# Gate and up projections of the experts taken by pairs of units, weights side by side

## The chip, the cores and the metric

The kernel runs on one core of one Trainium2 chip. The metric is the device time of one execution in microseconds (us); the median of several runs counts. Engines are named as in the profile: PE is the matrix engine TensorE (PEld its weight loads), DVE is VectorE, ACT is ScalarE, POOL is GpSimd, SP is SyncE, which issues the DMAs here.

## The reference

Two layers of a decoder trunk over 16 + 256 tokens of width 1024. The change touches only the last sub-layer, a top-2-of-8 expert SwiGLU:

```python
def swiglu(h, w_gate, w_up, w_down):
    return (jax.nn.silu(h @ w_gate) * (h @ w_up)) @ w_down

def moe_swiglu(h, router_w, w_gate, w_up, w_down):
    ...
    for e in range(N_EXPERTS):
        out = out + gates[..., e:e + 1].astype(h.dtype) * swiglu(h, w_gate[e], w_up[e], w_down[e])
    return out
```

There are 8 experts, each with gate and up matrices of 1024 x 3584 and a down matrix of 3584 x 1024, all float32. The weights, read once, are most of the kernel's traffic.

## The kernel before

The expert stage is a loop over 56 steps `s` (8 experts `e`, 7 slices `f` of 512 hidden columns). Each expert works on up to 128 gathered tokens. The tokens are the stationary operand of every product (`XG[e]`, tile `xq`) and the weights are the moving one, 512 columns at a time. To come near float32 accuracy from products in the faster type fp32r, each operand is split in a high and a low part, and three products are summed: high x high, high x low, low x high.

The weights come through `Stream`. A DMA brings a `raw` tile of 128 x 2048 (1 MB) from `wm`, in the order in which the host laid them out. A **unit** is half of such a tile, 128 x 1024, that is two chunks `k` of 512 columns. For each unit ACT makes the high part `whi` (`high`, L141) and DVE the low part `wlo` (`split`, L153: raw minus high). The pool `hl` holds four buffers of each kind (`HLB = 4`), so the high part of unit n+4 is written where that of unit n stood and waits for PE's last product that reads it. `unit(u)` sees to it that u and the three units behind it are split, and returns u's two parts. It is called where PE's products are written; the calls set the order in which casts and subtractions stand among the other work of ACT and DVE. In this stage the order of each engine's instructions is that of the program text (`manual_schedule`).

One step before the change, for s > 0:

- `gate_up(s, 0)`: gate, four units, six products for each (two chunks, each L1495, L1496, L1497), into one PSUM tile `gu`.
- ACT: Silu of that tile into `sg` (L1601).
- `transp(hcur)`: four transposes of the step before (L1505), ACT copies them to `hh` (L1508, high part), DVE makes `hlw` (L1509, low part).
- `gate_up(s, 1)`: up, four units, into a second `gu`; DVE multiplies `sg` by it (L1606).
- `down(s - 1, ...)` twice: four units, L1524 to L1526, into the tiles `yp0` and `yp1`, which live for the seven steps of an expert.

At an expert's end `unload` copies `yp0` and `yp1` out (L1536 on ACT, L1537 on DVE), and `combine` adds them to the tokens in the next step. `bg` takes up such pieces of background work between products. In the last step of all, `st.depth` falls from 4 to 3, and ACT loads a table for the final root (`tabs`, L1609).

Of the kernel before, what the change touches and what calls it, by code (L numbers as in the profile page):

```python
# [8 lines left out]
F32 = mybir.dt.float32  # L9
# [3 lines left out]
AF = mybir.ActivationFunctionType  # L13
ALU = mybir.AluOpType
PSUM = bass.MemoryType.PSUM

P = 128
D = 1024
ND = 8
# [17 lines left out]
TW = 2048  # L37
UW = 1024
# [42 lines left out]
class Stream:  # L81
# [71 lines left out]
        nc.vector.tensor_tensor(lo, w, hi.bitcast(F32), op=ALU.subtract)  # L153
        self.units[u] = (hi, lo)

    def unit(self, u, last=None):
        v, n = u, 0
        while n < self.depth and v * UW < self.n * TW:
            if not self.is_raw(v):
                if self.lim < self.n and v // self.per >= NWF and v // self.per not in self.raw:  # L160
                    break
                self.split(v)
                n += 1
            v += 1
        for k in [k for k in self.units if k < u]:
            del self.units[k]
        for k in [k for k in self.raw if k < u // self.per - R1 - R2]:
            del self.raw[k]
        return self.units[u]
# [6 lines left out]
def trunk(ctx: ExitStack, tc: tile.TileContext, xt, pv, pw, cst, gfin, wf, wm, out, dbg=None):  # L176
    nc = tc.nc
    pe, act, dve, pool = nc.tensor, nc.scalar, nc.vector, nc.gpsimd
# [3 lines left out]
    ring1 = ctx.enter_context(tc.tile_pool(name="ring1", bufs=R1))  # L182
# [9 lines left out]
    def psum(tag, name):  # L192
        t = ps.tile([P, 512], F32, name=name, tag=tag)
        return t

    st = Stream(nc, ring1, hl, wf, wm)
# [115 lines left out]
    def bg(n):  # L312
        for _ in range(min(n, len(fill))):
            fill.pop(0)()
# [10 lines left out]
    with ExitStack() as mx:  # L325
# [52 lines left out]
        us = [fraw(B_S5, 8, raw_x(xf), NT)]  # L378
# [511 lines left out]
        for b in range(2):  # L890
            sg = slot(f"sg{b}")
# [31 lines left out]
    with ExitStack() as fx:  # L923
# [24 lines left out]
        for k0, k1 in ((0, 6), (6, 8)):  # L948
            for w in range(2):
                (hi, lo), o = first[w]  # L950
                for k in range(k0, k1):
                    c = k * P
# [54 lines left out]
    with ExitStack() as gx:  # L1007
# [329 lines left out]
        for m in range(8):  # L1337
            if m < 4:
                o = accs[m]
# [145 lines left out]
    def unit_base(s):  # L1485

        return 8 * s + 4 * max(0, s - 1)

    def gate_up(s, w):
        e = s // NF  # L1490
        o = psum("mm", "gu")
        for k in range(ND):
            hi, lo = st.unit(UM + unit_base(s) + 4 * w + k // 2)
            c = slice((k % 2) * 512, (k % 2) * 512 + 512)
            pe.matmul(o, XG[e][:, 0, k], hi[:, c], start=(k == 0), stop=False)  # L1495
            pe.matmul(o, XG[e][:, 0, k], lo[:, c], start=False, stop=False)  # L1496
            pe.matmul(o, XG[e][:, 1, k], hi[:, c], start=False, stop=(k == ND - 1))  # L1497
            if k % 2:
                bg(1)
        return o  # L1500

    def transp(h):
        tp = psum("x", "etp")
# [77 lines left out]
    for s in range(E * NF + 1):  # L1581
        last = s == E * NF
        e, f = divmod(s, NF)
        if s == 1:
            weigh()
        if s == 2 * NF:
            gft = const.tile([P, D], F32, name="gft", tag="gft")
            nc.sync.dma_start(gft, gfin[0:1].to_broadcast([P, D]))
        if s == E * NF - 1:
            st.depth = 3  # L1590
        if f == 1 and e:
            fill += [lambda d=d, i=i: combine(e - 1, d, i) for d in range(2) for i in range(2)]
        if e % 2 and e + 1 < E and f == 3:
            choose(e + 1)
            gather(e + 1)
        if f == 2 and not last:
            turn_choice(e)
        if not last:
            og = gate_up(s, 0)
            sg = ew.tile([P, 512], F32, name="sg")  # L1600
            act.activation(sg, og, AF.Silu)  # L1601
        if s and not last:
            ht = transp(hcur)
        if not last:
            ou = gate_up(s, 1)
            dve.tensor_tensor(sg, sg, ou, op=ALU.mult)  # L1606
            hcur = sg
        if s == E * NF - 1:
            act.activation(tabs, epst, AF.Sqrt)  # L1609
            down(s - 1, *ht, 0)  # L1610
            hn = transp(hcur)
            down(s - 1, *ht, 1)
            ht = hn
        elif last:
            down(s - 1, *ht, 0)
            unload(E - 1, 0)
            fill.append(lambda: [combine(E - 1, 0, i) for i in range(2)])
            down(s - 1, *ht, 1)
            gains(0)
            Ys[E - 1, 1] = [ew.tile([P, 512], F32, name="Yf", tag="xq2", bufs=1)]  # L1620
            act.activation(Ys[E - 1, 1][0], yps[E - 1, 1], AF.Copy)
        elif s:
            for d in range(2):
                down(s - 1, *ht, d)
                if s % NF == 0:
                    unload(e - 1, d)
# [10 lines left out]
    with tc.If(cnt > CAP):  # L1637
        pos2 = ep.tile([P, 2, 8], F32, name="pos2")
        dve.tensor_scalar(pos2, pos, -float(CAP), None, op0=ALU.add)
        for e in range(E):  # L1640
            ohs = ep.tile([P, 2, CAP], F32R, name="ohs2", tag="ohs", bufs=1)
            for i in range(2):
                dve.tensor_scalar(ohs[:, i], css("iota"), pos2[:, i, e:e + 1], None, op0=ALU.is_equal)
            tp = psum("x", "ohtp")
            for i in range(2):
                pe.transpose(tp[:, i * P:(i + 1) * P], ohs[:, i].bitcast(F32), ident)
            oht = ew.tile([P, 2, P], F32, name="oht2", tag="oht", bufs=1)
            act.activation(oht.rearrange("p i t -> p (i t)"), tp[:, :2 * P], AF.Copy)
            xe = ew.tile([P, 2, ND, CAP], F32, name="xe2", tag=f"xq{e % 2}", bufs=1)[:, 0]
            for k in range(ND):  # L1650
                gp_ = psum("x", "gp_")
                o = gp_[:, :CAP]
                for j in range(4):
                    w = (XL if j > 1 else XH)[:, j % 2, k * P:(k + 1) * P]
                    pe.matmul(o, w, ohs[:, j % 2], start=(j == 0), stop=(j == 3))
                act.activation(xe[:, k], o, AF.Copy)
            yp2 = [psum("mm", f"yp{d}") for d in range(2)]
            for f in range(NF):
                s = e * NF + f
                tg = unit_base(s) // 2  # L1660
                pair = []
                for w in range(2):
                    o = psum("mm", "gu")
                    for k in range(ND):
                        if k % 4 == 0:
                            rw = ring1.tile([P, TW], F32, name="raw2", tag="raw")
                            nc.sync.dma_start(rw, wm[tg + 2 * w + k // 4])
                        pe.matmul(o, xe[:, k], rw[:, (k % 4) * 512:(k % 4) * 512 + 512], start=(k == 0), stop=(k == 7))
                    pair.append(o)
                sg = ew.tile([P, 512], F32, name="sg")  # L1670
                act.activation(sg, pair[0], AF.Silu)
                dve.tensor_tensor(sg, sg, pair[1], op=ALU.mult)
                tp = psum("x", "etp")
                for j in range(4):
                    pe.transpose(tp[:, j * P:(j + 1) * P], sg[:, j * P:(j + 1) * P], ident)
                hh = ew.tile([P, 4, P], F32, name="hh2", tag="hh")
                act.activation(hh.rearrange("p j c -> p (j c)"), tp, AF.Copy)
                td = (unit_base(s + 1) + 8 if s + 1 < E * NF else unit_base(s + 1)) // 2
                for d in range(2):
                    rw = ring1.tile([P, TW], F32, name="raw3", tag="raw")  # L1680
                    nc.sync.dma_start(rw, wm[td + d])
                    for j in range(4):
                        pe.matmul(yp2[d], hh[:, j], rw[:, 512 * j:512 * j + 512], start=(f == 0 and j == 0),
                                  stop=(f == NF - 1 and j == 3))
            Y = ew.tile([P, 4, 512], F32, name="Y2", tag="Y", bufs=1)[:, :2]
            for d in range(2):
                act.activation(Y[:, d], yp2[d], AF.Copy)
            for i in range(2):
                for d in range(2):
                    o = psum("x", "cmb")  # L1690
                    pe.matmul(o, oht[:, i], Y[:, d], start=True, stop=True)
                    a = X[:, i, 512 * d:512 * d + 512]
                    dve.scalar_tensor_tensor(a, o, gat[:, i, e:e + 1], a, op0=ALU.mult, op1=ALU.add)

        sqs = ew.tile([P, 4, 512], F32, name="sqs", tag="xq0", bufs=1)
        gains(0)
        for d in range(2):
            squares(d)
        finish()


def _layout(inp):
# [85 lines left out]
    i = 0  # L1788
    for s in range(n + 1):
        if s < n:  # L1790
            wm[i:i + 2] = g[s]
            wm[i + 2:i + 4] = u[s]
            i += 4
        if s > 0:
            wm[i:i + 2] = d[s - 1]
            i += 2
# [40 lines left out]
```

## Time and profile before

| | |
|---|---|
| median of 3 runs | 1548.89 us (1548.7 to 1555.63) |
| the profiled execution's own time | 1549.66 us |
| span of its profile, first to last instruction | 1547.9 us |
| PE / PEld / DVE / ACT busy share of the span | 99% / 85% / 83% / 68% |
| DMA, mean over the span | 280 GB/s |
| first and last product of the expert stage begin at | 557.5 us and 1534.3 us |

The busy shares are averages over stages with different limits. The expert stage takes the last 64% of the span; it is the only one that the change touches, so it is read by itself below. A matmul's duration in the profile contains its drain, which lies under the next one: a row of 0.39 us does not mean that the next product starts 0.39 us later.

### The profile page before, as it was taken

The page shows a single profiled execution, that of the slowest core. Times are in us where ns is not written, and L with a number is a line of the kernel's source. Part 1 is how long each engine was busy: PE and PEld are TensorE (multiplying, and loading weights), DVE is VectorE, ACT ScalarE, POOL GpSimd, SP SyncE. Part 2 cuts the span into 40 slices and gives each one's busy share as a digit, 9 for nine tenths or more (in the row PEclk, how much of TensorE's full clock was granted, in tenths as well). Part 3 has the DMA queues.
Part 4 walks back from the last instruction along what each step waited for, and adds up shares of the span by engine and source line. Part 5 has one row for each costly group of instructions (what it writes and reads, how often), then busy time and mean ns, then how long its engine had stood idle before and what let it go on. Part 6 is the DMA issues. An engine that isn't in the chain of part 4 may idle for free.

```text
span 1547.9 us, 21948 instructions
## 1 busy us (share of the span) xinstructions
PE 1525.1 (99%) x8346; PEld 1321.7 (85%) x8346; DVE 1287.5 (83%) x1445; ACT 1048.5 (68%) x1265; POOL 134.9 (9%) x248
## 2 busy tenths in 40 slices
PE   9998999999999999999999999999999999999997
PEld 7888999999899988888888888888888888888885
DVE  6677676655595689999999999999999999999996
ACT  3345654444552587878787887777887787787875
POOL 8870100001200200000000000000000000000000
PEclk9999999999999999999999999999999999999998
DMA  7433555455336768999899999999999999999960
GB/s 249 140 100 113 170 188 185 166 176 179 109 137 238 279 250 322 372 364 355 337 382 347 375 372 353 342 377 355 364 363 368 347 352 354 376 375 361 356 240 29
DMA packets 69041, 434.09 MB, mean 280 GB/s; under 512 B 14400, under 2 KB 14784, under 8 KB 17216
## 3 DMA queue, kind: packets, MB, share of 16 engines
q1 hardware_dynamic: 68784, 432.35, 74.9%
q8 instruction: 67, 1.10, 0.3%
q14 instruction: 46, 0.38, 0.1%
q10 hardware_dynamic: 144, 0.26, 0.0%
HBM read 430.32 MB, written 1.05 MB: 279 GB/s over the span
## 4 chain that ended last, share of the span: by engine, by line
PE 86%; DVE 1%; issue 1%; ACT 1%; POOL 0%; DVEq 0%; ACTq 0%; POOLq 0%
PE gu L1495 13%; PE gu L1497 13%; PE gu L1496 13%; PE yp L1524 7%; PE yp L1526 7%; PE yp L1525 7%; PE acc L231 6%; PE acc L232 6%; PE acc L233 6%; PE etp L1505 2%; PE sc L1106 1%; PE acc L252 1%; PE wo L231 1%; PE wo L233 1%; PE wo L232 1%
## 5 line engine op out<-in xcount | busy, mean ns | idle before, releaser
L153 DVE TENSOR_TENSOR wlo<-raw,whi 128x1024 fp32r<-128x1024 f32 x788 | 948.9, 1223 | 124.0 <-ACT whi L141 86.6
L141 ACT ACTIVATE whi<-raw 128x1024 fp32r<-128x1024 f32 x788 | 825.7, 1060 | 277.3 <-PE gu L1497 100.6
L1495 PE MATMUL gu<-whi,xq 128*128 128x512 f32 x896 | 357.6, 399 | 0.6 <-ACT xq L1427 0.6
L1497 PE MATMUL gu<-whi,xq 128*128 128x512 f32 x896 | 351.4, 392 | 0.0
L1496 PE MATMUL gu<-wlo,xq 128*128 128x512 f32 x896 | 349.8, 390 | 0.0
L1497 PEld LDWEIGHTS gu<-whi,xq 128*128 128x128 f32 x896 | 168.2, 188 | 38.4 <-DVE xq L1428 0.2
L1496 PEld LDWEIGHTS gu<-wlo,xq 128*128 128x128 f32 x896 | 168.5, 188 | 34.7 <-DVE wlo L153 0.4
L1495 PEld LDWEIGHTS gu<-whi,xq 128*128 128x128 f32 x896 | 168.5, 188 | 33.9 <-ACT xq L1427 0.8
L1524 PE MATMUL yp<-whi,hh 128*128 128x512 f32 x448 | 176.0, 393 | 0.0
L1526 PE MATMUL yp<-whi,hlw 128*128 128x512 f32 x448 | 175.3, 391 | 0.0
L1525 PE MATMUL yp<-wlo,hh 128*128 128x512 f32 x448 | 174.8, 390 | 0.0
L231 PE MATMUL acc<-xg,whi 128*128 128x272 f32 (+1 forms) x576 | 167.9, 292 | 0.0
L233 PE MATMUL acc<-xg,wlo 128*128 128x272 f32 (+1 forms) x576 | 166.0, 288 | 0.4 <-DVE wlo L153 0.4
L232 PE MATMUL acc<-xg,whi 128*128 128x272 f32 (+1 forms) x576 | 165.3, 287 | 0.5 <-DVE xg L266 0.5
L231 PEld LDWEIGHTS acc<-xg,whi 128*128 128x128 f32 x576 | 108.5, 188 | 1.1 <-issue 0.6
L232 PEld LDWEIGHTS acc<-xg,whi 128*128 128x128 f32 x576 | 108.5, 188 | 0.9 <-DVE xg L266 0.7
L233 PEld LDWEIGHTS acc<-xg,wlo 128*128 128x128 f32 x576 | 108.4, 188 | 0.7 <-DVE wlo L153 0.6
L1526 PEld LDWEIGHTS yp<-whi,hlw 128*128 128x128 f32 x448 | 84.1, 188 | 19.0
L1525 PEld LDWEIGHTS yp<-wlo,hh 128*128 128x128 f32 x448 | 84.1, 188 | 18.5 <-DVE wlo L153 0.3
L1524 PEld LDWEIGHTS yp<-whi,hh 128*128 128x128 f32 x448 | 84.2, 188 | 17.4
L1566 POOL TENSOR_TENSOR ys<-X,gft 128x512 f32<-128x512 f32 x1 | 1.6, 1594 | 988.1 <-DVE X L1547 988.1
L252 PE MATMUL acc<-xfn,raw 128*128 128x272 f32 x320 | 78.2, 401 | 1.4 <-DMA raw<-in_wf_dram 0.7
(528 smaller groups left out, 1725.4 us busy)
## 6 DMA issues: line engine op xcount, KB each, us to landing
raw<-in_wm_dram SPq DMA_DIRECT2D x334, 1024.0 KB, 6.0
raw<-in_wf_dram SPq DMA_DIRECT2D x70, 1024.0 KB, 4.9
raw<-in_wm_dram SPq DMA_DIRECT2D x4, 512.0 KB, 6.4
hT<-in_xt_dram SPq DMA_DIRECT2D x4, 272.0 KB, 4.9
raw<-in_wf_dram SPq DMA_DIRECT2D x2, 512.0 KB, 5.3
out_dram<-ys SPq DMA_DIRECT2D x3, 256.0 KB, 4.1
KT<-k SPq DMA_DIRECT2D x10, 64.0 KB, 2.2
U<-uA SPq DMA_DIRECT2D x16, 34.0 KB, 2.1
```

The costliest lines, as they stand in the source:

```text
L141: self.nc.scalar.activation(hi, self.tile(i)[:, j * UW:(j + 1) * UW], AF.Copy)
L153: nc.vector.tensor_tensor(lo, w, hi.bitcast(F32), op=ALU.subtract)
L231: pe.matmul(o, wh, xh, start=start, stop=False)
L232: pe.matmul(o, wh, xl, start=False, stop=False)
L233: pe.matmul(o, wl, xh, start=False, stop=stop)
L252: pe.matmul(o, w[:, c:c + P], xs(k), start=(k == 0), stop=(k == nblk_k - 1))
L1495: pe.matmul(o, XG[e][:, 0, k], hi[:, c], start=(k == 0), stop=False)
L1496: pe.matmul(o, XG[e][:, 0, k], lo[:, c], start=False, stop=False)
L1497: pe.matmul(o, XG[e][:, 1, k], hi[:, c], start=False, stop=(k == ND - 1))
L1524: pe.matmul(o, hh[:, j], hi[:, c], start=(f == 0 and j == 0), stop=False)
L1525: pe.matmul(o, hh[:, j], lo[:, c], start=False, stop=False)
L1526: pe.matmul(o, hlw[:, j], hi[:, c], start=False, stop=(f == NF - 1 and j == 3))
```

## The change

Gate and up are no longer computed one after the other. `gate_up(s, os, k0, k1)` takes the chunks k0 to k1 of both: for each chunk four products with the tokens' high part (gate high, gate low, up high, up low), then two with the low part. So two units, one of gate and one of up, are in use at once. They are called a **pair** here: p0 to p3 in each step, twelve products each, u0 to u3 of down behind them, six products each. The host lays gate and up halves side by side, so that a pair is one `raw` tile; the DMAs keep their number and size. Both PSUM tiles `gu` are taken at the step's start. The transposes now stand between p1 and p2 (before: between gate and up, at the same distance from both ends). The Silu of the gate moves from the middle of the step to its end, straight before DVE's product. `unit(u + 1, 1)` counts the first unit as done, so that with four buffers the two units behind a pair are split while it is in use. The last hunk but one does the same in a branch for overfull experts, which did not run.

```diff
-    def unit(self, u, last=None):
-        v, n = u, 0
+    def unit(self, u, n=0):
+        v = u
         while n < self.depth and v * UW < self.n * TW:
...
-    def gate_up(s, w):
+    def gate_up(s, os, k0, k1):
+
         e = s // NF
-        o = psum("mm", "gu")
-        for k in range(ND):
-            hi, lo = st.unit(UM + unit_base(s) + 4 * w + k // 2)
+        for k in range(k0, k1):
+            if k % 2 == 0:
+                u = UM + unit_base(s) + k
+                us = [st.unit(u), st.unit(u + 1, 1)]
             c = slice((k % 2) * 512, (k % 2) * 512 + 512)
-            pe.matmul(o, XG[e][:, 0, k], hi[:, c], start=(k == 0), stop=False)
-            pe.matmul(o, XG[e][:, 0, k], lo[:, c], start=False, stop=False)
-            pe.matmul(o, XG[e][:, 1, k], hi[:, c], start=False, stop=(k == ND - 1))
-            if k % 2:
-                bg(1)
-        return o
+            for o, (hi, lo) in zip(os, us):
+                pe.matmul(o, XG[e][:, 0, k], hi[:, c], start=(k == 0), stop=False)
+                pe.matmul(o, XG[e][:, 0, k], lo[:, c], start=False, stop=False)
+            for o, (hi, lo) in zip(os, us):
+                pe.matmul(o, XG[e][:, 1, k], hi[:, c], start=False, stop=(k == ND - 1))
+            bg(1)
...
         if not last:
-            og = gate_up(s, 0)
-            sg = ew.tile([P, 512], F32, name="sg")
-            act.activation(sg, og, AF.Silu)
+            gu = [psum("mm", "gu") for _ in range(2)]
+            gate_up(s, gu, 0, 4)
         if s and not last:
             ht = transp(hcur)
         if not last:
-            ou = gate_up(s, 1)
-            dve.tensor_tensor(sg, sg, ou, op=ALU.mult)
+            gate_up(s, gu, 4, 8)
+            sg = ew.tile([P, 512], F32, name="sg")
+            act.activation(sg, gu[0], AF.Silu)
+            dve.tensor_tensor(sg, sg, gu[1], op=ALU.mult)
             hcur = sg
...
-            wm[i:i + 2] = g[s]
-            wm[i + 2:i + 4] = u[s]
+            for h in range(4):
+                c = slice((h % 2) * UW, (h % 2) * UW + UW)
+                wm[i + h, :, :UW] = g[s, h // 2, :, c]
+                wm[i + h, :, UW:] = u[s, h // 2, :, c]
             i += 4
```

The order on ACT, around the copy `hh` of one step in the middle of the stage, before (numbers tell buffers of one name apart):

```order
L141 ACTIVATE whi_8656<-raw_8339 128x1024
L141 ACTIVATE whi_8666<-raw_8339 128x1024
L141 ACTIVATE whi_8678<-raw_8362 128x1024
L1601 ACTIVATE sg_8688<-gu_8643 128x512
L1508 ACTIVATE hh_8695<-etp_8690 128x512
L141 ACTIVATE whi_8700<-raw_8362 128x1024
L141 ACTIVATE whi_8712<-raw_8384 128x1024
L141 ACTIVATE whi_8722<-raw_8384 128x1024
```

and the same step of the changed kernel:

```order
L141 ACTIVATE whi_8663<-raw_8339 128x1024
L141 ACTIVATE whi_8667<-raw_8339 128x1024
L1510 ACTIVATE hh_8688<-etp_8683 128x512
L141 ACTIVATE whi_8694<-raw_8369 128x1024
L141 ACTIVATE whi_8698<-raw_8369 128x1024
L141 ACTIVATE whi_8716<-raw_8400 128x1024
L141 ACTIVATE whi_8720<-raw_8400 128x1024
L1608 ACTIVATE sg_8736<-gu_8643 128x512
```

Before, one cast of gate and up stands behind `hh` (`whi_8700`, the last unit of up) and the next ones are of down. Now both casts of p3 stand behind it (`whi_8694`, `whi_8698`), and the Silu stands behind the casts of u0 and u1, where it waits for the end of p3 with the casts of u2 and later behind it. On DVE the subtractions stand in the order of these casts, `hlw` in the place of `hh`.

On PE, of the same step, what reads the part that was cast behind `hh`. Before, four transposes, six products of unit 8656, six of unit 8666, and then:

```order
L1495 MATMUL gu_8699<-whi_8678,xq_7095 128x512
L1496 MATMUL gu_8699<-wlo_8680,xq_7095 128x512
L1497 MATMUL gu_8699<-whi_8678,xq_7095 128x512
L1495 MATMUL gu_8699<-whi_8678,xq_7095 128x512
L1496 MATMUL gu_8699<-wlo_8680,xq_7095 128x512
L1497 MATMUL gu_8699<-whi_8678,xq_7095 128x512
L1495 MATMUL gu_8699<-whi_8700,xq_7095 128x512
L1496 MATMUL gu_8699<-wlo_8702,xq_7095 128x512
```

In the changed kernel, four transposes, the first six products of p2, and then:

```order
L1498 MATMUL gu_8643<-whi_8663,xq_7095 128x512
L1499 MATMUL gu_8643<-wlo_8665,xq_7095 128x512
L1498 MATMUL gu_8644<-whi_8667,xq_7095 128x512
L1499 MATMUL gu_8644<-wlo_8669,xq_7095 128x512
L1501 MATMUL gu_8643<-whi_8663,xq_7095 128x512
L1501 MATMUL gu_8644<-whi_8667,xq_7095 128x512
L1498 MATMUL gu_8643<-whi_8694,xq_7095 128x512
L1499 MATMUL gu_8643<-wlo_8696,xq_7095 128x512
L1498 MATMUL gu_8644<-whi_8698,xq_7095 128x512
L1499 MATMUL gu_8644<-wlo_8700,xq_7095 128x512
```

The first part cast behind `hh` was read by the 19th product after the transposes and is now read by the 13th; the second, and its low part, by the 15th and 16th, where before it was read from the 25th on, in down.

In the last step, s = 55, on ACT, before:

```order
L1508 ACTIVATE hh<-etp 128x512
L141 ACTIVATE whi<-raw 128x1024 x4
L1609 ACT_TABLE_LOAD
L1609 ACTIVATE tabs<-epst 128x1
L141 ACTIVATE whi<-raw 128x1024 x2
```

and now:

```order
L1510 ACTIVATE hh<-etp 128x512
L141 ACTIVATE whi<-raw 128x1024 x4
L1608 ACTIVATE sg<-gu 128x512
L1612 ACT_TABLE_LOAD
L1612 ACTIVATE tabs<-epst 128x1
L141 ACTIVATE whi<-raw 128x1024 x3
```

The table load has moved behind the Silu at the step's end, and the three casts behind it are those of u1, u2 and u3; the four casts behind `hh` are those of up's half of p2, of p3, and of u0.

## Rows read from the trace of the kernel before

**Rows 1.** The page: the span, and weight loads of two lines

```profile
span 1547.9 us, 21948 instructions
...
L1496 PEld LDWEIGHTS gu<-wlo,xq 128*128 128x128 f32 x896 | 168.5, 188 | 34.7 <-DVE wlo L153 0.4
L1495 PEld LDWEIGHTS gu<-whi,xq 128*128 128x128 f32 x896 | 168.5, 188 | 33.9 <-ACT xq L1427 0.8
```

**Rows 2.** Busy time by stretch: stretch, its length, engines' busy us, PEclk, DMA, GB/s

```profile
800.00:900.00 100.00, 100.00 (x452) 82.10 (x451) 93.64 (x88) 79.96 (x85) 0.00 (x0) 1.00 0.98 367
```

**Rows 3.** Who waited for whom, 700 to 1500 us: us, times, longest us

```profile
ACT whi L141 <- PE gu L1497: 84.1, 260, 0.9
```

**Rows 4.** The same for SP's queue, 700 to 1500 us

```profile
SPq L116 <- DVE wlo L153: 627.4, 252, 4.2
```

**Rows 5.** Timeline of PE over one step: start, us, instruction

```profile
904.27 0.39 PE L1496 MATMUL gu<-wlo,xq 128*128 128x512 f32 x1
904.50 0.40 PE L1497 MATMUL gu<-whi,xq 128*128 128x512 f32 x1
...
905.09 0.47 PE L1495 MATMUL gu<-whi,xq 128*128 128x512 f32 x1
905.40 0.39 PE L1496 MATMUL gu<-wlo,xq 128*128 128x512 f32 x1
905.62 0.39 PE L1497 MATMUL gu<-whi,xq 128*128 128x512 f32 x1
905.85 0.39 PE L1495 MATMUL gu<-whi,xq 128*128 128x512 f32 x1
906.08 0.39 PE L1496 MATMUL gu<-wlo,xq 128*128 128x512 f32 x1
...
910.43 0.39 PE L1497 MATMUL gu<-whi,xq 128*128 128x512 f32 x1
```

**Rows 6.** Timeline of ACT, the same step and the next one's start

```profile
904.93 0.60 ACT L1601 ACTIVATE sg<-gu 128x512 f32<-128x512 f32 x1 [0.31 <-PE gu L1497]
905.42 0.59 ACT L1508 ACTIVATE hh<-etp 128x512 fp32r<-128x512 f32 x1
905.90 2.01 ACT L141 ACTIVATE whi<-raw 128x1024 fp32r<-128x1024 f32 x2
...
910.86 1.06 ACT L141 ACTIVATE whi<-raw 128x1024 fp32r<-128x1024 f32 x1 [0.31 <-PE gu L1497]
...
921.85 0.60 ACT L1601 ACTIVATE sg<-gu 128x512 f32<-128x512 f32 x1 [0.31 <-PE gu L1497]
```

**Rows 7.** Timeline of DVE, the same stretch

```profile
906.05 0.69 DVE L1509 TENSOR_TENSOR hlw<-etp,hh 128x512 fp32r<-128x512 f32 x1 [0.18 <-ACT hh L1508]
907.00 4.81 DVE L153 TENSOR_TENSOR wlo<-raw,whi 128x1024 fp32r<-128x1024 f32 x4 [0.26 <-ACT whi L141]
911.72 0.68 DVE L1606 TENSOR_TENSOR sg<-sg,gu 128x512 f32<-128x512 f32 x1
912.32 10.48 DVE L153 TENSOR_TENSOR wlo<-raw,whi 128x1024 fp32r<-128x1024 f32 x8
...
923.91 2.36 DVE L153 TENSOR_TENSOR wlo<-raw,whi 128x1024 fp32r<-128x1024 f32 x2 [0.25 <-ACT whi L141]
```

**Rows 8.** Timeline of DVE at the stage's start: the low part of the first tokens

```profile
557.45 0.42 DVE L1428 TENSOR_TENSOR xq<-gp__5591,xq 128x256 fp32r<-128x256 f32 x1 [0.78 <-ACT xq L1427]
```

**Rows 9.** Timeline of PEld, the load that waited for it

```profile
557.93 0.19 PEld L1497 LDWEIGHTS gu<-whi,xq 128*128 128x128 f32 x1 [0.16 <-DVE xq L1428]
```

**Rows 10.** Timeline of PE shortly before: products that change the PSUM bank every second time

```profile
554.78 0.40 PE L1421 MATMUL gp__5591<-ohs,XL 128*128 128x256 f32 x2
555.02 0.40 PE L1421 MATMUL gp__5594<-ohs,XL 128*128 128x256 f32 x2
```

**Rows 11.** Groups by line, 700 to 1500 us: the copies at an expert's end

```profile
L1537 DVE TENSOR_TENSOR Y<-yp,Y 128x512 fp32r<-128x512 f32 x12 | 8.2, 683 | 0.0
```

**Rows 12.** Timeline of ACT in the last step: the table load

```profile
1520.78 1.28 ACT L1609 ACT_TABLE_LOAD   x1
```

More of the change, by code (lines that the diff above doesn't have):

```diff
@@ L1660, in trunk @@
                 tg = unit_base(s) // 2
[L1661 to L1669, printed above, removed]
+                pair = [psum("mm", "gu") for _ in range(2)]
+                for k in range(ND):
+                    if k % 2 == 0:
+                        rw = ring1.tile([P, TW], F32, name="raw2", tag="raw")
+                        nc.sync.dma_start(rw, wm[tg + k // 2])
+                    for w, o in enumerate(pair):
+                        c = w * UW + (k % 2) * 512
+                        pe.matmul(o, xe[:, k], rw[:, c:c + 512], start=(k == 0), stop=(k == 7))
                 sg = ew.tile([P, 512], F32, name="sg")
```

## The prediction

> **What bounds the kernel now.** I read the busy time by stretch first. In a stretch from the middle of the expert stage PE is busy for 100 of 100 us, at a granted clock of 1.00, its upper level of 2.4 GHz, DVE for 94 and ACT for 80 [rows 2]. Busy is not yet bound, so the waits come next: ACT's casts wait for PE to let go of a buffer [rows 3], and SP waits 627 us in total for DVE to free a tile [rows 4]; PE waits for nobody. PE's own timeline then gives its pace: from the product at 905.40 to that at 910.43 there are 22, one in 0.2286 us [rows 5], against 0.2133 us for 512 columns at 2.4 GHz. A step takes 16.92 us, from one Silu to the next (904.93, 921.85) [rows 6]. So PE bounds the stage, and any wait of PE is lost for good.
>
> How near are the others? On DVE the second of two queued subtractions ends 2.36 us after the first began, one alone takes 1.22, so each takes a slot of 1.14; `hlw` or the product of `sg` takes one of 0.60 (911.72 to 912.32) [rows 7]. A step has 12 and 2 of them: 14.9 of 16.92 us. No engine is overfull. What the change can cost is latency: how long after PE's last use of a buffer the next unit is ready in it.
>
> **The latency in terms.** From the start of PE's last product on a unit (910.43) to the cast that it lets go (910.86): 0.43 us [rows 5, 6]. From a cast's start (905.90) to its subtraction's (907.00): 1.10 [rows 6, 7]. A slot: 1.14; the last subtraction in full: 1.22. From DVE's end (557.87) to PE's weight load that waited for it (557.93): 0.06 [rows 8, 9].
>
> **Products, transposes, DMAs: 0.** Their number does not change. The `raw` tiles keep size and order, and each is still freed by its second subtraction; SP stands waiting for such slots [rows 4], so tiles come early, and a later slot only shortens that lead. Both `gu` tiles are needed at the step's start; the Silu and the product that free them end about 2 us after p3 (0.43 + 0.60 + 0.68 and some queue), and down's 24 products, 5.5 us, cover that. Without this cover, p0 would wait the 2 us.
>
> **Pairs in a row: about 0.** With both units of a pair in use, p's buffers go to the pair after next. Its second low part is ready 0.43 + 1.10 + 1.14 + 1.22 + 0.06 = 3.95 us after p's 11th product began, and is wanted by the 4th product of that pair, 17 products later: 3.89. The four transposes (905.09 instead of 904.73, so 0.36 us) lie between p0 and p2, which makes this free there. Two pairs run into the next points.
>
> **p3 waits for the copy `hh`: 0.90 us a step.** ACT and DVE do their work in the written order, and both of p3's units now stand behind `hh` and `hlw`. All needed instants stand in the trace, since up to the transposes nothing moves. After the last product of p1 (904.50) `hh` starts at 905.42 and the first two casts behind it run from 905.90 for 2.01 us [rows 6]; their subtractions begin at 907.00 and 908.14, the second ends at 909.36, so PE can have it at 909.42 [rows 7]. Before, only the first was gate or up work, wanted by the 20th product after the transposes; the second was of down. Now p2 begins at 905.09, its second product at 905.40 [rows 5], its twelfth at 905.40 + 10 x 0.2286 = 907.69, and p3's first to fourth at 907.91, 908.14, 908.37 and 908.60. The second waits for the first low part until 908.28, the fourth for the second until 909.42: 0.82 us late. The product after a break follows at 0.31 instead of 0.23 (905.09, 905.40): 0.08 more. Sum 0.90. What is queued behind the waiting product is all of PE: down, and the Silu.
>
> **The step's end: 0.17 us a step.** p3's 11th product moves to 909.42 + 0.31 + 6 x 0.2286 = 911.10. The Silu follows at 911.53, and u2's cast, behind it on ACT, 0.49 later (904.93 to 905.42 [rows 6]) at 912.02. DVE then does u2, u3 and the next p0's two units without a pause: 912.02 + 1.10 + 3 x 1.14 + 1.22 + 0.06 = 917.82. PE wants the last one for p0's 4th product, 29 after the 11th of p3: 917.73. So 0.09 late, and 0.08 for the break. Before, the Silu stood in mid-step, and this chain did not exist. It is a small difference of long sums; the bounds below vary it.
>
> **An expert's end: 0.60 more, 7 times.** There DVE's copy L1537, 0.68 us long [rows 11], stands between p0's two units and takes a slot like `hlw`: 4.2 us in all.
>
> **The last step: about 5 us.** With a lead of three, even p2's second unit stands behind `hh`. Its low part is there at 908.28, and p2's 4th product wants it at 905.40 + 2 x 0.2286 = 905.86: 2.42 us late. p3's 11th product then starts at 912.70, the Silu at 913.13, and the table load of 1.28 us [rows 12] now stands between it and u1's cast, which starts at 913.62 + 1.28 = 914.90; its low part is there at 914.90 + 1.10 + 1.22 + 0.06 = 917.28, wanted by u1's second product at 914.76: 2.52 late. With two breaks 5.1 us.
>
> **The sum.** Steps 1 to 54 lose 1.07 us each, 57.8 us; 4.2 and 5.1 make 67.1. In three steps tokens for the next experts are gathered between the products of p2, p3 and down; these extra products fill some of the wait, up to 0.90 each, so I take 2 off: 65. The profiled execution took 1549.66 us itself, the median is 0.8 less: 1548.9 + 65 = **1614 us**, 4.2% slower.
>
> **Bounds.** Down: no time to release PE and no break after a wait. Then p3 loses 0.76 and the step's end 0.03: 0.79 x 54 + 4.2 + 5.1 - 2.7 = 49, so 1598. Up: the four subtractions from 907.00 took 4.81 us, a slot of (4.81 - 1.22) / 3 = 1.20 [rows 7], partly because the later ones waited for casts. With 1.20 throughout p3 loses 0.06 more and the step's end 0.18: 1.31 x 54 + 10 = 81, so 1630.
>
> **Rivals.** *Holding the tokens' high part saves its loading.* Four products in a row now share a stationary operand. But L1495 and L1496 shared theirs before: each has 896 weight loads of 188 ns all the same [rows 1], and L1496 follows L1495 (905.85 to 906.08) in 0.23 us as L1495 follows L1497 (905.62 to 905.85) with other weights [rows 5]. If loads fell away now, no more than 0.2286 - 0.2133 = 0.015 us could go on four of six of the 2688 products: 27 us. PE would then reach p3's 4th product 0.16 us earlier and wait that much longer, 9 us in all: 1614 - 18 = 1596, slower still. The loss of 65 us is 0.024 us for each of those products, more than the 0.015 there is, so no hold alone can decide for faster. The Trainium skill ("TensorE: Matmul & The Clock Gate", step-by-step) has it that one loads once and multiplies repeatedly, and gives 216 ns for back-to-back products of 512 columns; by an estimate from that page 2688 products at 216 instead of 229 ns would save about 35 us. The rows show no product at that pace.
>
> *p3's casts come in time (the other side).* Their buffers are free 0.43 us after p1's 11th and 12th products (904.27, 904.50), at 904.70 and 904.93. If ACT took these casts ahead of `hh`, the second would be done by 906.7, its subtraction, behind the first's or `hlw`, about 908.2, ahead of 908.60: no wait at p3, none at the step's end, 1549 to 1560, with the last step's loss. It decides from 0.82 us of the chain of 4.92. Against it: ACT's order puts them behind, and before, the first cast behind `hh` also had its buffer free at 904.93 and started at 905.90.
>
> *PE slows down in changing banks.* Four products now change the PSUM tile every second time. The Trainium skill (same page, on a second failure mode, "psum-queue depth-cycling") says that cycling through banks leaves small gaps in which the clock falls. By rows: at the lower level 512 columns take 0.427 us, and 2688 products would cost 533 us more, about 2080 us. Against it: just before the stage products of 256 columns changed tile every second time and two took 0.24 us (554.78, 555.02), the pace of full clock [rows 10].
>
> **Chances.** Forecast, within its bounds or a little beyond, 0.82; waits larger than these bounds, to 1650, 0.07; a saved load, 0.04; casts in time, 0.06, of which 0.02 together with a saved load, 1549 - 27 = 1522; slower clock, 0.01. 0.5% is about what a measurement can tell here. Faster 0.02, same 0.04, slower 0.94. The range takes the bounds and 4 us on each side: 1594 to 1634.
>
> **What the profile after would show.** Right: L1499 has idle time before it with DVE's `wlo` as releaser, 40 to 60 us in all, in about one place or two of each step; a step of 17.8 to 18.2 us; DVE's share falls to 88%; L1498, L1499 and L1501 have 896 loads each. Wrong, if PE still runs without a pause, if the pace in p0 to p2 differs from 0.229, or if the waits stand at p1 or p2.

## The result, and the profile after

The changed kernel takes **1615.82 us**, the median of 6 runs (1613.55 to 1623.62), against 1549.08 (1548.36 to 1555.63) for the kernel before: a ratio of 1.043, 95% interval [1.041, 1.0451]. The forecast was 1614, in a range of 1594 to 1634. The profiled execution took 1614.64 us.

The page of the changed kernel answers to [rows 1]. Behind the bar stand busy time and mean of one, then the idle time ahead of the line and who ended most of it:

```profile
span 1612.9 us, 22000 instructions
...
L1499 PE MATMUL gu<-wlo,xq 128*128 128x512 f32 x896 | 368.3, 411 | 25.4 <-DVE wlo L153 25.4
...
L1499 PEld LDWEIGHTS gu<-wlo,xq 128*128 128x128 f32 x896 | 168.6, 188 | 109.5 <-DVE wlo L153 80.5
L1498 PEld LDWEIGHTS gu<-whi,xq 128*128 128x128 f32 x896 | 168.8, 188 | 36.3 <-ACT xq L1427 2.0
L1501 PEld LDWEIGHTS gu<-whi,xq 128*128 128x128 f32 x896 | 169.0, 189 | 33.8
```

There are still 896 loads in each of the three lines, 188 to 189 ns each: holding the tokens removed none. What is new is that L1499, the products with the low part of the weights, waits for DVE's subtraction. PE's own row shows 25.4 us of it and the row of the weight loads 80.5. The second is the fuller count. A product's modelled end lies 0.4 us or more behind its start, while its successor can start after 0.23, so the first part of a wait is covered by the end of the product ahead.

The busy time of a stretch in the middle of the stage, to set beside [rows 2], with the same columns:

```profile
900.00:1000.00 100.00, 97.48 (x426) 76.00 (x425) 87.09 (x84) 70.36 (x78) 0.00 (x0) 1.00 0.89 343
```

PE has lost a few per cent, DVE has fallen from 94 to 87 and ACT from 80 to 70: no engine is overfull, all wait for one another. The clock stays at 1.00.

Now the place in the step. The weight loads of PE around p3, where the number in brackets is the wait and its releaser:

```profile
910.51 0.19 PEld L1499 LDWEIGHTS gu<-wlo,xq 128*128 128x128 f32 x1 [0.35 <-DVE wlo L153]
...
911.64 0.19 PEld L1499 LDWEIGHTS gu<-wlo,xq 128*128 128x128 f32 x1 [0.84 <-DVE wlo L153]
```

and PE's products of the same step, to set beside [rows 5]; the first row of transposes and the last give the step's length:

```profile
889.05 0.60 PE L1507 MATMUL etp<-cs,sg 128*128 128x128 f32 x4
...
906.56 0.62 PE L1501 MATMUL gu<-whi,xq 128*128 128x512 f32 x2
907.02 0.60 PE L1507 MATMUL etp<-cs,sg 128*128 128x128 f32 x4
907.37 0.47 PE L1498 MATMUL gu<-whi,xq 128*128 128x512 f32 x1
...
910.20 0.40 PE L1498 MATMUL gu<-whi,xq 128*128 128x512 f32 x1
910.51 0.50 PE L1499 MATMUL gu<-wlo,xq 128*128 128x512 f32 x1
910.85 0.39 PE L1498 MATMUL gu<-whi,xq 128*128 128x512 f32 x1
911.65 0.51 PE L1499 MATMUL gu<-wlo,xq 128*128 128x512 f32 x1 [0.41 <-DVE wlo L153]
911.99 0.63 PE L1501 MATMUL gu<-whi,xq 128*128 128x512 f32 x2
...
919.34 0.39 PE L1498 MATMUL gu<-whi,xq 128*128 128x512 f32 x1
...
920.06 0.50 PE L1499 MATMUL gu<-wlo,xq 128*128 128x512 f32 x1
920.40 0.62 PE L1501 MATMUL gu<-whi,xq 128*128 128x512 f32 x2
...
924.99 0.60 PE L1507 MATMUL etp<-cs,sg 128*128 128x128 f32 x4
```

From one group of transposes to the next a step takes 17.97 us here (907.02 to 924.99; 17.98 over the stage), before 16.92. From p3's first product to its fifth it is 1.79 us (910.20 to 911.99) where four products at 0.2286 take 0.91: 0.88 lost. At the next p0 it is 1.06 (919.34 to 920.40): 0.15 lost. The rest of the step runs at the old pace, without a wait at p1 or p2.

The releasers stand on ACT and DVE, to set beside [rows 6, 7]:

```profile
907.65 0.60 ACT L1510 ACTIVATE hh<-etp 128x512 fp32r<-128x512 f32 x1 [1.40 <-PE etp L1507]
908.14 4.03 ACT L141 ACTIVATE whi<-raw 128x1024 fp32r<-128x1024 f32 x4
```

```profile
908.28 0.69 DVE L1511 TENSOR_TENSOR hlw<-etp,hh 128x512 fp32r<-128x512 f32 x1 [0.59 <-ACT hh L1510]
909.23 4.63 DVE L153 TENSOR_TENSOR wlo<-raw,whi 128x1024 fp32r<-128x1024 f32 x4 [0.26 <-ACT whi L141]
```

ACT stands idle for 1.40 us before `hh`, though p1's last product began at 906.79 (906.56 + 0.23) and its buffers were free soon after: it waits in its written order for the transposes. Only then come p3's two casts, and DVE's second subtraction ends about 911.59 (909.23 + 1.14 + 1.22), 0.05 us ahead of the load at 911.64.

**Where the 65.0 us of the span went** (1612.9 - 1547.9), counted from one group of transposes to the next:

| part | before, us | after, us | times | sum, us |
|---|---|---|---|---|
| intervals between transposes, all | 940.95 | 997.4 | 54 | +56.5 |
| of these: ordinary, on average | 16.98 | 18.00 | 44 | +1.02 each |
| of these: at an expert's end | 18.81 | 20.46 | 7 | +1.65 each |
| of these: with tokens gathered | 20.77 | 20.77 | 3 | 0 |
| first step, to its first transposes | 17.27 | 18.79 | 1 | +1.5 |
| last interval | 8.94 | 16.62 | 1 | +7.7 |
| the stage's start and what follows the last transposes | | | | -0.7 |

The commonest ordinary step went from 16.92 to 17.98 us, 1.06 more. The first interval and those behind an expert's end, 17.15 to 17.18 before, lost less (18.03 to 18.16), so the average is 1.02.

### The profile page after: what moved, and what is told of

Same layout as the page of the kernel before. It is cut to its first block, busy times and chain, and to the rows that moved or that the text cites. A ratio compares the mean times of both kernels' runs of the same rounds, so it can differ in the third digit from the quotient of the medians.

```text
span 1612.9 us, 22000 instructions
## 1 busy us (share of the span) xinstructions
PE 1562.3 (97%) x8346; PEld 1312.1 (81%) x8346; DVE 1274.4 (79%) x1445; ACT 1015.2 (63%) x1265; POOL 134.9 (8%) x248
## 4 chain that ended last, share of the span: by engine, by line
PE 70%; DVE 12%; ACT 5%; issue 4%; ACTq 0%; DVEq 0%
PE gu L1499 10%; DVE wlo L153 10%; PE gu L1501 10%; PE gu L1498 8%; PE yp L1527 6%; PE yp L1528 6%; PE yp L1526 6%; PE acc L232 5%; PE acc L231 5%; PE acc L233 5%; ACT whi L141 4%; PE etp L1507 2%; PE sc L1106 1%; PE acc L252 1%; PE go L231 1%
## 5 line engine op out<-in xcount | busy, mean ns | idle before, releaser
L153 DVE TENSOR_TENSOR wlo<-raw,whi 128x1024 fp32r<-128x1024 f32 x788 | 922.7, 1221 | 148.2 <-ACT whi L141 147.3
L141 ACT ACTIVATE whi<-raw 128x1024 fp32r<-128x1024 f32 x788 | 793.9, 1053 | 224.1 <-PE acc L232 99.2
L1499 PE MATMUL gu<-wlo,xq 128*128 128x512 f32 x896 | 368.3, 411 | 25.4 <-DVE wlo L153 25.4
L1498 PE MATMUL gu<-whi,xq 128*128 128x512 f32 x896 | 358.1, 400 | 3.0 <-ACT xq L1427 1.8
L1501 PE MATMUL gu<-whi,xq 128*128 128x512 f32 x896 | 279.7, 393 | 0.0
L1499 PEld LDWEIGHTS gu<-wlo,xq 128*128 128x128 f32 x896 | 168.6, 188 | 109.5 <-DVE wlo L153 80.5
L1510 ACT ACTIVATE hh<-etp 128x512 fp32r<-128x512 f32 x56 | 33.5, 598 | 88.6 <-PE etp L1507 88.3
```

The source lines that it names most:

```text
L141: self.nc.scalar.activation(hi, self.tile(i)[:, j * UW:(j + 1) * UW], AF.Copy)
```

## Experiments

The theory of the prediction: each step loses 0.9 us because both units of p3 stand behind `hh` on ACT and are wanted at once, and some 0.2 us because the Silu at the step's end stands ahead of the next casts. Rivals: the weights' new layout or the Silu's new place costs by itself; the change of PSUM tile or the held operand costs (or saves) on PE; the buffers, not the order, are what is short.

**1. The copies behind p3's casts.** In the changed kernel, `hh` and `hlw` stand behind both casts and subtractions of p3.

```diff
             if k % 2 == 0:
                 us = [st.unit(u), st.unit(u + 1, 1)]
+                while later:
+                    later.pop()()
...
-        act.activation(hh..., tp, AF.Copy)
-        dve.tensor_tensor(hlw..., op=ALU.subtract)
+        later.append(copies)
```

> The changed kernel with one thing moved: the two copies of the transposes (hh on ACT, hlw on DVE) stand behind the casts and subtractions of p3 instead of ahead of them. Theory (p3 waits because its casts stand behind hh): p3's wait of about 0.9 us a step goes, a step falls from 17.98 to about 17.1 us, the wait at the next p0 stays; 1563 us, 1557 to 1570. Rival (PE is slower in itself when four products share an operand and the PSUM tile changes every second time, or pairs starve each other anywhere): no change, 1616.

Measured: 1570.27 us (1567.44 to 1572.34), ratio to before 1.0122 [1.0104, 1.0141]. An ordinary step takes 17.12 us: 0.86 of the 1.06 are gone. p3 runs without a pause, and what stays is the wait at p0: in this kernel its third, fourth and fifth product start at 908.74, 909.01 and 909.35, which is 0.15 over the pace. All waits of PE's weight loads for `wlo` in this stage (us in total, times, longest):

```profile
PEld gu L1503 <- DVE wlo L153: 18.6, 47, 0.9
```

In the changed kernel this row read, over the same stretch:

```profile
PEld gu L1499 <- DVE wlo L153: 74.5, 140, 0.9
```

The 54 intervals are together 43.9 us shorter, and the last one is 3.7 us shorter (12.90); but in the profiled execution the stage began 4.5 us later, at 561.0 instead of 556.5. So 43.1 remain; the profiled executions differ by 43.0 us (1614.64 and 1571.62), the medians by 45.6. That later start is why the time lies just above the 1557 to 1570 that were expected. The time was lost at the kernel's beginning, which the edit does not touch: PE is busy for 94.9 and 94.2 of the first two 100 us, where the changed kernel shows 98.4 and 96.5. Its cause stays open.

**2. The copy twice.** The suspected wait made longer: ACT runs `hh` two times.

```diff
-        act.activation(hh..., tp, AF.Copy)
+        for _ in range(2):
+            act.activation(hh..., tp, AF.Copy)
```

> The changed kernel with hh copied twice by ACT, one instruction more ahead of p3's casts in each step. Theory: p3's second low part comes 0.48 us later, and as its wait lies wholly on PE's path the step grows by as much: 55 x 0.48 = 26 us, 1642 (1636 to 1648). Rival (the wait has another cause, and ACT, busy 72%, has room): 1616 to 1620.

Measured: 1650.43 us (1649.24 to 1650.92), ratio 1.0641 [1.0624, 1.0659]. That is 2.4 us above the range. The ordinary step grew by 0.63 us, to 18.61; all intervals, the last one included, grew by 34.0 us together, of the 34.6 between the medians of this kernel and the changed one. The two copies on ACT:

```profile
957.51 1.23 ACT L1511 ACTIVATE hh<-etp 128x512 fp32r<-128x512 f32 x2 [1.40 <-PE etp L1507]
958.63 2.94 ACT L141 ACTIVATE whi<-raw 128x1024 fp32r<-128x1024 f32 x3
```

Two of them take 1.23 us where one took 0.60, so the second costs 0.63 and not the 0.48 that I took from the distance of `hh` to the cast behind it. The size was off by that, and the mechanism holds: what was put between `hh` and p3's casts, PE paid in full in an ordinary step.

**3. Unit by unit in the new layout.** The weights stay side by side and the Silu stays at the end, but each unit's six products run in a row, gate's and up's units taking turns. No operand is held, and two units are no longer in use at once.

```diff
-        for k in range(k0, k1):
...
+        for k in range(k0, k1, 2):
+            for w, o in enumerate(os):
+                hi, lo = st.unit(UM + unit_base(s) + k + w)
+                for i in range(2):
+                    pe.matmul(o, XG[e][:, 0, k + i], hi[:, c], ...)
+                    pe.matmul(o, XG[e][:, 0, k + i], lo[:, c], ...)
+                    pe.matmul(o, XG[e][:, 1, k + i], hi[:, c], ...)
+                bg(1)
```

> The new layout, the Silu at the step's end and the transposes between p1 and p2 stay, but a pair's two units are used one after the other, six products each, so that no operand is held and each buffer is let go after its six products. Theory: neither wait is left, since the order of casts around hh is that of the kernel before and the gate is done six products ahead of the step's end; 1549 to 1553. Rival (the layout, or the Silu's place, costs): 1565 or more, with waits at p0.

Measured: 1550.07 us (1547.39 to 1555.68), ratio 1.0004 [0.9992, 1.0016]. Two groups of transposes of this kernel, 16.95 us apart as before:

```profile
995.12 0.60 PE L1505 MATMUL etp<-cs,sg 128*128 128x128 f32 x4
...
1012.07 0.60 PE L1505 MATMUL etp<-cs,sg 128*128 128x128 f32 x4
```

So the layout, both `gu` tiles at the step's start and the Silu's new place cost nothing by themselves; even the last interval is back at 8.89 us, and the first step takes 17.07. The whole loss hangs on having both units of a pair in use at once.

**4. A fifth buffer.** The changed kernel with five pairs of `whi` and `wlo` instead of four. To make room, a ring of the stage ahead went from three tiles to two.

```diff
-R1 = 3
+R1 = 2
...
-HLB = 4
+HLB = 5
```

> The changed kernel with five buffers of high and low parts instead of four, so that one cast of p3 stands ahead of hh and each unit is split one earlier; the room comes from the ring of raw tiles, 2 instead of 3, which may cost something in the stages ahead of the experts. Theory: p3's second low part is then the first behind hh, ready at 908.28 in the times of the step worked out, wanted at 908.60, and the chain of the step's end has 1.14 us less: no waits, a step of 16.92 us in the expert stage, 1549 to 1556 if the stages ahead keep their time. Rival (PE slower in itself): steps of 17.98 us stay.

Measured: 1569.22 us (1568.32 to 1569.82), ratio 1.012 [1.0103, 1.0137], so not what was expected, but the steps are. The steps take 16.92, 18.81 and 20.77 us, as before, all 54 intervals together 940.97 us against 940.95, and the waits of gate's and up's weight loads for `wlo` have come down to one, in the last step:

```profile
PEld gu L1499 <- DVE wlo L153: 1.1, 1, 1.1
```

What is left is 11.0 us by which the stage starts later (568.5 against 557.5: PE, in the stages ahead, is busy for 94.2 of the first 100 us instead of 97.6, and for 91.4 of the second instead of 95.2; the smaller ring is the likely cause, but it was not tried without the fifth buffer) and a last interval of 16.55 us, 7.6 more than before. Together 18.6, of the 18.9 by which the median lies above that of the kernel before, run beside it (1550.3). With a buffer more p3's casts no longer need p1's buffers, and the order on ACT no longer matters: the loss takes both, the order and the shortage.

**5. One operand for all.** The kernel before, in which every product of gate and up uses one and the same 128x128 piece of the tokens.

```diff
-            pe.matmul(o, XG[e][:, 0, k], hi[:, c], ...)
-            pe.matmul(o, XG[e][:, 0, k], lo[:, c], ...)
-            pe.matmul(o, XG[e][:, 1, k], hi[:, c], ...)
+            pe.matmul(o, XG[e][:, 0, 0], hi[:, c], ...)
+            pe.matmul(o, XG[e][:, 0, 0], lo[:, c], ...)
+            pe.matmul(o, XG[e][:, 0, 0], hi[:, c], ...)
```

> The kernel before, with its own order, but all gate and up products of an expert use one and the same stationary operand, the high part of the tokens' first chunk (the sums are then others; the count, sizes and order of instructions are not). 48 products in a row share it, against two in a row before. Rival (holding an operand saves part of its load): up to 0.015 us on nearly all 2688 products, 40 us, 1509. Theory (each product loads its operand again, whether it is the same or not): 1549, with 896 loads on each line and 0.229 us from product to product.

Measured: 1549.41 us (1548.11 to 1555.48), ratio 1.0008 [0.9995, 1.0022]. Its weight loads on the page:

```profile
L1496 PEld LDWEIGHTS gu<-wlo,xq 128*128 128x128 f32 x896 | 168.5, 188 | 34.7 <-DVE wlo L153 0.4
L1495 PEld LDWEIGHTS gu<-whi,xq 128*128 128x128 f32 x896 | 168.5, 188 | 35.1 <-ACT xq L1427 2.0
```

Each product still has its load, and the pace is the same. A hold saves nothing here, of four products in a row or of 24 (the expectation's 48 counts across the four transposes between gate and up). No run issued fewer loads, so what leaving a load out would save is not shown.

**6. p3 alone unit by unit.** In the changed kernel, p0 to p2 as they are, p3's two units one after the other.

```diff
-        for k in range(k0, k1):
+        for k in range(k0, min(k1, 6)):
...
+        if k1 == 8:
+            for w, o in enumerate(os):
+                hi, lo = st.unit(UM + unit_base(s) + 6 + w)
+                for k in (6, 7):
+                    (the three products of chunk k)
+                bg(1)
```

> The changed kernel with p3 alone taken unit by unit: six gate products, then six of up; p0 to p2 hold the operand as before. Theory: p3's second low part is then wanted by the 8th product instead of the 4th, later than it is ready, and the gate is done six products before the step's end, which shortens the chain over the Silu by more than a microsecond. Only the wait of p3's second product for the first low part stays, 0.2 us with its break; a step of 17.1 us; with the last step as it is 1567 us (1562 to 1572). Rival (it is the number of pairs that costs): three of four pairs stay, so three quarters of the loss, 1599.

Measured: 1567.56 us (1566.9 to 1573.53), ratio 1.013 [1.0106, 1.0153]; a step of 17.12 us, as in the first experiment. One wait a step is left of the weight loads for `wlo`:

```profile
PEld gu L1509 <- DVE wlo L153: 17.1, 51, 0.4
```

p0 to p2 still take turns between two PSUM tiles and still hold the operand, so that is not what costs. What costs 0.86 us is that p3's second unit is wanted two products after its first, when six would be time enough. The wait that stays is not the one of the first experiment. It stands at p3's second product, whose low part comes a little late as before:

```profile
912.88 0.40 PE L1508 MATMUL gu<-whi,xq 128*128 128x512 f32 x1
913.17 0.50 PE L1509 MATMUL gu<-wlo,xq 128*128 128x512 f32 x1
913.51 0.39 PE L1510 MATMUL gu<-whi,xq 128*128 128x512 f32 x1
```

p0 now runs at its pace (921.29, 921.52, 921.75, 921.98, 922.21). Gate's sum is complete six products before up's in this kernel, where it was one before, so the Silu need not wait for the step's last product; that this is why p0 is in time was not tried by itself.

**7. The last step.** In the changed kernel, the lead stays at four units and the table load moves from the last step into the down products that follow it.

```diff
-        if s == E * NF - 1:
-            st.depth = 3
...
-            act.activation(tabs, epst, AF.Sqrt)
+    (the same line, between the two halves of the last down)
```

> The changed kernel with its last step mended: the lead stays at four units there, and the table load for the root stands behind the last down products instead of behind the Silu. Theory: the two waits of that step (for p2's second unit and for u1) go, and with them the stretch at half clock that followed; the other steps stay; about 6.5 us less, 1609 (1607 to 1612). If the half clock came from something else, the last step keeps 2 to 3 us.

Measured: 1607.7 us (1606.97 to 1611.73), ratio 1.0385 [1.0363, 1.0407]. The steps stay at 17.98, and the last interval falls from 16.62 to 9.55 us:

```profile
1572.56 0.60 PE L1507 MATMUL etp<-cs,sg 128*128 128x128 f32 x4
...
1582.11 0.60 PE L1507 MATMUL etp<-cs,sg 128*128 128x128 f32 x4
```

Those are 7.1 us, and the medians differ by 8.1. So nearly all of the last interval's excess is of these two causes, which were not tried apart. What stands above the 8.68 us that this interval takes without a break (experiment 8) is p3's ordinary wait, which this kernel has in its last step too (four products from 1575.75 to 1577.53, 0.87 over the pace).

**8. All three remedies.** The changed kernel with experiments 1, 6 and 7 together; p0 to p2 are still products of pairs.

```diff
+ the copies put off (experiment 1)
+ p3 unit by unit (experiment 6)
+ lead and table load of the last step (experiment 7)
```

> All three together: the copies hh and hlw behind p3's casts, p3 unit by unit, the last step mended. p0 to p2 still hold the tokens' high part for four products in a row. Theory: no wait is left, PE runs through at 0.229 us a product; the time of the kernel before, 1549 (1547 to 1552), same. If holding or the alternation of PSUM tiles had a price or a gain of its own, it would stand here alone: 2016 of the 2688 products are in pairs, so 1 ns on each is 2 us.

Measured: 1553.18 us (1551.88 to 1556.27, 12 runs), ratio 1.0024 [1.0013, 1.0035]: 4.1 us above before, 1.2 above the range. An ordinary step takes 16.92 again:

```profile
905.66 0.60 PE L1520 MATMUL etp<-cs,sg 128*128 128x128 f32 x4
...
922.58 0.60 PE L1520 MATMUL etp<-cs,sg 128*128 128x128 f32 x4
```

and the last interval is 8.68. Left are an expert's end, 19.21 instead of 18.81 us, 7 times (2.8), and the first step, 18.58 instead of 17.27 (1.3): together with the last interval 3.8 of the 4.1. At an expert's end DVE's copy (L1559 in this kernel, L1537 before) lies ahead of the subtractions that p0 wants; DVE and then the load that waits:

```profile
933.11 0.68 DVE L1559 TENSOR_TENSOR Y<-yp,Y 128x512 fp32r<-128x512 f32 x1
933.71 2.35 DVE L153 TENSOR_TENSOR wlo<-raw,whi 128x1024 fp32r<-128x1024 f32 x2
```

```profile
934.98 0.19 PEld L1503 LDWEIGHTS gu<-wlo,xq 128*128 128x128 f32 x1 [0.55 <-DVE wlo L153]
```

It does not beat the kernel before, nor does anything else here: PE runs all but without a pause there, and no version has a step shorter than 16.9 us.

## Why the prediction was right, point by point

**p3's wait, 0.90 a step: right, in place, cause and size.** 0.88 us were lost from p3's first to its fifth product. `hh` started 0.86 us after p1's last product (forecast 0.92) and the second low part was at hand 4.85 us after it (forecast 4.92), each link close to its row of before. Experiments 1 and 6 take away 0.86 us by the two sides of it, the order on ACT and the time of the demand; experiment 2 adds to it what it adds to ACT; experiment 4 removes it by a buffer. One thing was told too simply. The wait is not one break of 0.82 and 0.08: there are two, at the second product (0.31) and the fourth (0.80), and the product after each follows in 0.34 instead of 0.23.

**The step's end, 0.17: right.** 0.15 lost at p0, and the first experiment, which mends p3 alone, leaves just this. In experiment 8 it is gone.

**An expert's end, 0.60 more: right.** 1.65 against 1.06 us in the commonest step, so 0.59, seven times. Experiment 8 keeps 0.40 of it when the rest is gone.

**Gather steps, 2 us back: mis-sized.** They lost nothing at all (20.77 as before), so three times 1.02, 3.1 us, came back: the extra products covered the whole wait.

**The last step, 5.1: mis-sized.** It cost 7.7. The two waits were there: PE's products in the last step of the changed kernel, first at p2 and then in down,

```profile
1573.42 0.40 PE L1499 MATMUL gu<-wlo,xq 128*128 128x512 f32 x1
1574.97 0.50 PE L1498 MATMUL gu<-whi,xq 128*128 128x512 f32 x1 [1.16 <-ACT whi L141]
1576.23 0.68 PE L1499 MATMUL gu<-wlo,xq 128*128 128x512 f32 x1 [0.76 <-DVE wlo L153]
...
1577.57 0.63 PE L1498 MATMUL gu<-whi,xq 128*128 128x512 f32 x1
1578.00 0.63 PE L1499 MATMUL gu<-wlo,xq 128*128 128x512 f32 x1
...
1583.87 0.40 PE L1528 MATMUL yp<-whi,hlw 128*128 128x512 f32 x1
1585.81 0.50 PE L1526 MATMUL yp<-whi,hh 128*128 128x512 f32 x1 [1.54 <-ACT whi L141]
1587.07 0.80 PE L1527 MATMUL yp<-wlo,hh 128*128 128x512 f32 x1 [0.76 <-DVE wlo L153]
```

p2 waits 1.32 and then 1.03 us longer than the pace (1573.42, 1574.97, 1576.23), together 2.35 of the 2.42 forecast. u1 waits 1.71 and 1.03, together 2.74 of 2.52. So the breaks make 5.09 of the 5.1 forecast. The term that the sum left out stands behind them: after each pair of breaks the products lie 0.43 us apart for a while, since the clock fell, as the last section shows. Nine products from 1576.23 to 1579.98 and five from 1587.07 to 1589.37 took 2.85 us more than at the pace. Together 7.9, which is what lies between 8.68 and 16.62; the kernel before had a short wait of its own there and took 8.94.

**The first step, not in the sum: 1.5 us.** It has no down behind p3, so the next step's p0 and p1 follow at once. PE's loads for p1 wait for subtractions in two places, and the products after 571.19 come at 572.00, 572.34, 573.14 and 573.48 where the pace gives 0.23: 1.4 us. ACT had the casts ready early, from 568.45, straight behind the Silu; DVE turned to them at 570.73 only, behind the product of `sg` and nine small operations on the gates (L1474 to L1481), which the kernel before runs as late after the stage's start (12.9 us, here 12.7) without a loss. The Silu's new place alone does not do it: experiment 3 has the Silu and the product of `sg` in the same places, its subtractions come as late (14.3 us after the stage's start, here 14.2), and its first step takes 17.07 us. With a fifth buffer (experiment 4) it takes 17.31. So here too it is the pair in use with four buffers that costs; the remedies at p3 do not reach it (18.58 in experiment 8).

**The sum** held because these errors cancel: 57.8 + 4.2 - 2 + 5.1 forecast, 56.5 + 1.5 + 7.7 - 0.7 measured. The 56.5 stand against 60.0 of the forecast; that the last and the first step cost 4.1 more than forecast made up for it, and this was luck. The mechanism does not rest on it.

**The rivals.** A saved load: experiment 5 shows none at all. The Trainium skill ("TensorE: Matmul & The Clock Gate", step-by-step) speaks of loading once and multiplying repeatedly; by the estimate of about 35 us from its 216 ns, experiment 5 would have come near 1514, and it measured 1549.41, with a load still issued for each product. Casts in time: the first experiment is what that rival described, and it gives 1570 instead of 1549 to 1560. p3 is in time, but p0 is not, since the chain from p3's 11th product over the Silu to p0 has a length of its own; the rival had it vanish along with p3's wait. A slower clock by changing banks: in experiment 8 p0 to p2 change the PSUM tile as in the changed kernel, at 16.92 us a step and a granted clock of 1.00 from 900 to 1000 us. The loss of clock of which the Trainium skill (same page, "psum-queue depth-cycling") tells was not seen with this pattern. The 0.427 us of that rival stand in no row ahead of the prediction; the last step of the changed kernel shows 0.43 at the lower level.

**What the profile should show.** Step, DVE's share (87 for 88%), 896 loads a line and the free p1 and p2 came out as written. The idle time of L1499, 40 to 60 us, did not: 25.4 on PE's row and 80.5 on that of its weight loads, for the reason told above. The true loss lies between the two.

## What to carry to other kernels

When two units of work are taken together, ask when the second is wanted, not only how much work there is: no engine here had more to do, and most of the 4.3% went because a part was wanted four products earlier than it need be and ACT, in its written order, delivered it behind a copy that waited for PE itself. Count from the last use of a buffer over each hand-off to the next use; a chain of 4.92 us against a demand at 4.10 was enough to forecast p3's loss as 0.90 us, where 0.88 was measured. And before products are regrouped to hold an operand, see in the profile whether products that share one already run any faster.

## What the runs showed of the hardware that was not expected

The granted clock fell after two breaks close together, and the slow products behind them cost 2.85 us on top of the 5.09 of the breaks. The windows of the changed kernel's last step (length, busy time of PE, PEld, DVE, ACT and POOL, granted clock, DMA):

```profile
1566.00:1570.00 4.00, 4.00 (x19) 3.08 (x18) 4.00 (x4) 2.08 (x3) 0.00 (x0) 1.00 0.00 0
1574.00:1578.00 4.00, 2.26 (x6) 1.57 (x7) 3.74 (x4) 2.81 (x3) 0.00 (x0) 0.80 0.00 2
1578.00:1580.00 2.00, 2.00 (x7) 1.57 (x6) 0.45 (x1) 0.06 (x1) 0.00 (x0) 0.55 0.00 0
1580.00:1584.00 4.00, 4.00 (x19) 3.18 (x17) 1.90 (x2) 2.29 (x3) 0.00 (x0) 1.00 0.00 0
1587.00:1590.00 3.00, 2.93 (x8) 2.35 (x9) 2.28 (x3) 0.65 (x1) 0.00 (x0) 0.50 0.00 0
```

After the two breaks up to 1576.23 it went to its lower level of 1.2 GHz and was back at 2.4 by 1580, with the products at 0.43 and then 0.23 us again; after the second two, up to 1587.07, it fell once more. The waits of an ordinary step, 0.6 us at the longest beyond the pace, leave it at 1.00. In the seventh experiment, which has no such breaks, the same stretch shows 1.00:

```profile
1574.00:1578.00 4.00, 3.60 (x16) 2.41 (x15) 3.75 (x4) 3.69 (x4) 0.00 (x0) 1.00 0.01 2
```

A second point: a wait of PE for a low part costs more than its length. The product behind the one that waited comes 0.34 us later instead of 0.23, at each of p3's two waits and at p0's (910.51 to 910.85, 911.65 to 911.99, 920.06 to 920.40), so two short waits are dearer than one. In these places the product's weight load starts together with it (911.64 and 911.65), while elsewhere a load starts 0.23 us ahead of its product. Whether the load is what the extra tenth of a microsecond goes on, no run here shows.
